# State products of a head in one group, its outputs in another: mLSTM and retention in a hybrid decoder step

## The chip, the cores and the metric

The kernel runs on one core of one Trainium2 chip. The metric is the time of one execution on the device in microseconds (us). Five engines work beside each other, each through a queue of its own in program order, and wait for each other by semaphores: PE (TensorE, the matrix multiplier; its weight loads are listed as PEld), DVE (VectorE), ACT (ScalarE), POOL (GpSimd) and SP (SyncE, which here issues nearly all DMAs).

## The reference, cut to what matters

One decoder layer is run for a prompt of 512 tokens and for 8 samples of 8 tokens, 576 token columns in all. The input is projected by a wide matrix; four token mixers (RWKV-7, sliding-window attention, mLSTM, retention: branches a, b, c, d) work on parts of the projection; each branch output is gated, multiplied by its own matrix `w_branch[i]`, weighted and summed, and one output projection and a layer norm follow. The change concerns the two mixers with a matrix state:

```python
# mLSTM, per chunk (decays, stabilisers and normalisers left out)
A = jnp.einsum('bqhd,bkhd->bhqk', qc, kc) * wts
num = jnp.einsum('bhqk,bkhv->bhqv', A, vc) + sc[..., None] * jnp.einsum('bqhd,bhdv->bhqv', qc, C)
C_new = s_old[..., None, None] * C + jnp.einsum('bhk,bkhd,bhkv->bhdv', wj, kc, vc)
...
# retention, per chunk
inner = jnp.einsum('bqhd,bkhd->bhqk', qc, kc) * decay_mat
o = (jnp.einsum('bhqk,bkhv->bqhv', inner, vc)
     + jnp.einsum('bqhd,bhdv->bqhv', qc, S) * q_dec.T[None, :, :, None])
S = c_dec[None, :, None, None] * S + jnp.einsum('bkhd,bkhv,hk->bhdv', kc, vc, k_dec)
...
# after the branches
for i, y_i in enumerate((y_a, y_b, y_c, y_d)):
    branch = (y_i * z[:, :, i]).astype(x.dtype) @ w_branch[i]
    merged = merged + gate[:, :, i] * branch
out = merged.astype(x.dtype) @ w_out
```

## The kernel before

**Stages.** The prompt's 512 tokens are cut into four chunks of 128; the samples' 64 tokens are a fifth. The large dense products run in blocks. A block of the input projection is 128 output rows by 576 tokens over 16 slices of the inner dimension; each slice takes six matmuls (a high and a low half of both operands, three products, times two column halves), so a block is 96 matmuls into the tile `psd`. A block of a branch product (`w_branch`) has 8 slices and 48 matmuls, also into `psd`; it is written w*n*_*c* here, with *n* the branch and *c* one of its 16 blocks. Ahead of each four slices ACT splits the weights (`wh`) and DVE takes the rest (`wl`), in three buffers each (line 1584 on).

The order of the stages is: branches a, b and c, beside which input blocks run; then `Seven` (line 1264), which computes the remaining input blocks in pairs by a seven-product scheme, into the tile `pmx`, 168 matmuls a pair in place of 2 x 96; then branch d, beside which the blocks of w0 and w1 run; then what is left of the 64 branch blocks; and last the output projection (`pso`).

**What sets the order.** PE takes its matmuls in program order. `S.pump(n)` (`pump`, in `hybrid_kernel`) puts *n* steps into PE's stream, each step one slice (six matmuls) of the dense block at hand, and lets every pending finishing piece advance by a step. The counts in the pump calls of `branch_c_heads`, `branch_d` and `head_out` therefore decide how much dense work stands between the small matmuls of a head, and how far the list `work` has come when a branch ends. When branch c ends, all input blocks but four that were not yet begun go to `Seven`; the number of pairs follows from that (`rest`, then `n = (len(names) - AFTER_SEVEN) // 2`). `S.need(x)` pumps until x is done. The order of instructions on ACT, DVE and SP is set when the program is built, by a scheduler that follows the dependences.

**A head.** Branch c has 8 heads in 4 pairs, branch d has 8 heads. A head computes scores (`k2` by `q2`, `kr` by `qr`), multiplies them by decays (`at`), and then, chunk by chunk: the output from the scores (`vt`, `at`), to which the state of the chunk before is added (`cn`, `qd` or `dst`, `qd`), an eviction by ACT into `o`, the state product (`vt`, `kt`), and the new state by DVE (`cn`, `dst`). Two pump steps stand at each chunk. In branch c the outputs use the array as 128x128, the state term as 64x128 and the state product as 128x64 (rows by columns). The fifth chunk follows, and `head_out` normalises `o` (DVE statistics, POOL's `pow`, DVE), pumps 10 steps and transposes the result (`c_ident`, `o`) for `y`, which goes to DRAM (`yd`).

**Rows of a branch.** Before w*n*_0 can run, `load_rows` must bring branch n's 8 rows from DRAM (`ya<-yd`, `yb<-zsd`, two buffers each), multiply them (DVE `ya`), and split them (ACT `yh`, DVE `yl`). Rows 0 to 2 of branch 1 are asked for at w0_8, the others at the end of w0; those of branch 2 are asked for right after branch d's code, whatever block is at hand:

```python
    branch_d(S)
    rows.mixing = False
    y2ctx = ctx.enter_context(ExitStack())
    y2 = y2ctx.enter_context(tc.tile_pool(name="y2", bufs=1, side="right", reuse_waits="tile"))
    load_rows(2, range(8), y2)
    while current or work or finishing:
        pump(1)
```

## Time and profile before

| what | us |
|---|---|
| median of 3 runs (3237.12 to 3242.02) | 3240.61 |
| the profiled execution | 3245.12 |
| its span, first to last instruction | 3243.4 |
| PE busy in the span | 3194.1 |
| DVE busy | 1916.4 |
| ACT busy | 1190.1 |
| mean granted clock of TensorE | 0.992 |

The profiled execution is 4.5 us above the median and 3.1 us above the slowest of the three runs; 1.7 us of its time lie outside the span. In the views a row with `x2` merges two instructions. A matrix multiplication of plain 32-bit operands appears as two matmuls in the trace, so a head's `vt,at` stands there as `x2`. In "idle before" and in the view of waits, the name behind the arrow is what ended the wait. The clock column gives the TensorE clock that was granted, 1.00 being full speed.

### The profile page before, as it was taken

To read this page: it belongs to the slowest core of one execution; us is meant where nothing else is said; L and a number is where in the kernel's file an instruction comes from. 1 tells how busy PE (TensorE), PEld (TensorE's weight loads), DVE (VectorE), ACT (ScalarE), POOL (GpSimd) and SP (SyncE) were. 2 spreads that over 40 slices of the span, in tenths; PEclk is the share of its full clock that TensorE was granted. 3 is DMA by queue.
4 is the path that set the end of the run, shared out by engine and by line. 5 is a ranking of instruction groups with operands and counts; after the bars stand their busy time and mean duration, and the time that the engine had idled before them with its cause. 6 is when DMAs were issued, how large, how long until landed. Compare 5 with 4: busy or idle time off the path is not lost.

```text
span 3243.4 us, 60432 instructions
## 1 busy us (share of the span) xinstructions
PE 3194.1 (98%) x24238; PEld 3055.5 (94%) x24238; DVE 1916.4 (59%) x3889; ACT 1190.1 (37%) x2453; POOL 361.2 (11%) x606
## 2 busy tenths in 40 slices
PE   8999999999999999999999999999999999899998
PEld 8999999999999999999999999999999999899886
DVE  5555655665543663566566666666665676555426
ACT  4333433333232443323244444444444232223211
POOL 0432243224301220000000000000000000000000
PEclk9999999999999999999999999999999999899999
DMA  5332322323234222432443333333335774554513
GB/s 161 100 90 82 98 79 81 93 85 92 80 98 138 81 89 90 142 111 87 152 131 123 122 120 124 121 124 123 117 124 175 242 228 149 165 173 130 184 60 111
DMA packets 185017, 395.19 MB, mean 122 GB/s; under 512 B 64472, under 2 KB 69336, under 8 KB 184144
## 3 DMA queue, kind: packets, MB, share of 16 engines
q1 hardware_dynamic: 184736, 391.32, 38.2%
q8 instruction: 191, 3.13, 0.4%
q14 instruction: 90, 0.74, 0.1%
HBM read 323.99 MB, written 65.59 MB: 120 GB/s over the span
## 4 chain that ended last, share of the span: by engine, by line
PE 92%; DMA 3%; DVE 3%; ACT 1%; issue 1%; SPq 0%; POOL 0%; ACTq 0%; DVEq 0%; POOLq 0%
PE psd L1484 47%; PE pmx L1484 26%; PE pm L1484 13%; PE pso L1532 6%; DMA xs<-in_xT 1%; DVE wl L1590 1%; DMA raw<-in_wi 1%; ACT wh L1589 0%; DMA ya<-yd 0%; DVE xk L1500 0%; DMA raw<-in_wo 0%; DVE tm L1500 0%; DVE e L1500 0%; DVE res L1500 0%; DMA raw<-in_wb 0%
## 5 line engine op out<-in xcount | busy, mean ns | idle before, releaser
L1590 DVE TENSOR_TENSOR wl<-raw,wh 128x512 fp32r<-128x512 f32 x740 | 535.3, 726 | 467.9 <-ACT wh L1589 452.8
L1589 ACT ACTIVATE wh<-raw 128x512 fp32r<-128x512 f32 x740 | 465.0, 630 | 921.3 <-PE psd L1484 691.3
L1484 PE MATMUL psd<-xh,wh 128*128 128x288 f32 (+2 forms) x3072 | 707.6, 312 | 9.8 <-ACT wh L1589 9.4
L1484 PE MATMUL psd<-xl,wh 128*128 128x288 f32 (+2 forms) x3072 | 660.2, 296 | 0.0
L1484 PE MATMUL psd<-xh,wl 128*128 128x288 f32 (+2 forms) x3072 | 659.3, 296 | 0.4 <-DVE wl L1590 0.4
L1484 PEld LDWEIGHTS psd<-xh,wh 128*128 128x128 f32 x3072 | 492.0, 189 | 38.4 <-issue 12.6
L1484 PEld LDWEIGHTS psd<-xh,wl 128*128 128x128 f32 x3072 | 504.4, 189 | 1.2 <-DVE wl L1590 1.0
L1484 PEld LDWEIGHTS psd<-xl,wh 128*128 128x128 f32 x3072 | 504.5, 189 | 0.0
L1484 PE MATMUL pmx<-xh,wl 128*128 128x288 f32 x1248 | 369.0, 296 | 3.5 <-DVE wl L1590 3.5
L1484 PE MATMUL pmx<-xl,wh 128*128 128x288 f32 x1248 | 368.8, 295 | 0.0
L1484 PE MATMUL pmx<-xh,wh 128*128 128x288 f32 x1248 | 368.8, 295 | 0.0
L1484 PE MATMUL pmx<-fh,wl 128*128 128x288 f32 x864 | 257.5, 298 | 0.0
L1484 PE MATMUL pmx<-fl,wh 128*128 128x288 f32 x864 | 255.4, 296 | 0.0
L1484 PE MATMUL pmx<-fh,wh 128*128 128x288 f32 x864 | 254.4, 294 | 0.0
L1484 PEld LDWEIGHTS pmx<-xh,wl 128*128 128x128 f32 x1248 | 235.9, 189 | 3.9 <-DVE wl L1590 3.9
L1484 PE MATMUL psd<-yh,wh 128*128 128x288 f32 x1024 | 227.2, 304 | 11.1 <-ACT yh L1500 8.8
L1484 PEld LDWEIGHTS pmx<-xh,wh 128*128 128x128 f32 x1248 | 236.0, 189 | 0.0
L1484 PEld LDWEIGHTS pmx<-xl,wh 128*128 128x128 f32 x1248 | 235.8, 189 | 0.0
L1484 PE MATMUL psd<-yl,wh 128*128 128x288 f32 x1024 | 221.3, 298 | 0.3 <-DVE yl L1500 0.3
L1484 PE MATMUL psd<-yh,wl 128*128 128x288 f32 x1024 | 221.2, 298 | 0.0
L1484 POOL TENSOR_TENSOR rstd<-rstd,mhalf 128x5 f32<-128x5 f32 (+1 forms) x24 | 37.5, 1565 | 1567.1 <-DVE rstd L1500 1567.1
L1484 PEld LDWEIGHTS psd<-yh,wh 128*128 128x128 f32 x1024 | 165.5, 191 | 14.4 <-ACT yh L1500 9.7
(384 smaller groups left out, 4957.1 us busy)
## 6 DMA issues: line engine op xcount, KB each, us to landing
raw<-in_wi SPq DMA_DIRECT2D x270, 512.0 KB
sraw<-in_wi SPq DMA_DIRECT2D x72, 512.0 KB
raw<-in_wb SPq DMA_DIRECT2D x64, 512.0 KB
gd<-zs SPq DMA_DIRECT2D x64, 288.0 KB
th<-gd SPq DMA_DIRECT2D x64, 288.0 KB
raw<-in_wo SPq DMA_DIRECT2D x32, 512.0 KB
zsd<-zs SPq DMA_DIRECT2D x32, 288.0 KB
ya<-yd SPq DMA_DIRECT2D x32, 288.0 KB
```

The costliest lines, as they stand in the source:

```text
L1484: ins = f(*a, **k).ins
L1532: PE.matmul(out=out, lhsT=lhsT, rhs=rhs, start=start, stop=stop)
L1589: a = nc.scalar.activation(out=wh, in_=src, func=ACTF.Copy)
L1590: b = nc.vector.tensor_tensor(out=wl, in0=src, in1=wh.bitcast(FP32), op=ALU.subtract)
```

## The change

In both branches the four state products of a head are issued as one group of matmuls, ahead of the outputs, into banks shared by several chunks; DVE then computes the four states in a row; after some pump steps the four outputs (with the state terms) are issued as a second group, and ACT evicts several chunks with one instruction (three and one in branch c, four in branch d). Branch d keeps a head's four states in one tile. The pump counts change with it: in branch c a head pumped 4, four times 2, and 10 in `head_out`, 22 in all, and now 2, 5, 2 and 10, or 19; in branch d it pumped 6, 1, 3, four times 2 and 10, 28 in all, and now 6, 1, 2, 4, 2 and 7, or 22.

```diff
 FILL_BONUS = 10
+FILL_HEAD = dict(c=10, d=7)
...
                 V.memset(at[64:P, 4, 0:64], 0.0)
-                S.pump(4)
+                S.pump(2)
+
+                ps = [pm() for _ in range(2)]
+                inc = [ps[c // 3][rs, 129 * (c % 3):129 * (c % 3) + 129] for c in range(4)]
+                for c in range(4):
+                    mm(inc[c], kt[:, c, rs], vt[:, c, e])
+                for c in range(4):
+                    pst = inc[c]
+                    if c:
+                        stt(cn[c][rs], cn[c - 1][rs], scb[rs, c * P + P - 1:c * P + P], pst, ALU.mult, ALU.add)
+                    else:
+                        V.tensor_copy(out=cn[c][rs], in_=pst)
+                S.pump(5)
+                ps = [pm() for _ in range(2)]
                 for c in range(4):
                     cs = slice(c * P, c * P + P)
-                    S.pump(2)
-                    po = pm()
-                    mm(po[:, 0:129], at[:, c], vt[:, c, e], stop=(c == 0))
+                    po = ps[c // 3][:, 129 * (c % 3):129 * (c % 3) + 129]
+                    mm(po, at[:, c], vt[:, c, e], stop=(c == 0))
                     if c:
-                        mm(po[:, 0:129], qd[rs, cs], cn[c - 1][rs], start=False)
-                    act(o[:, c], po[:, 0:129])
-                    pst = pm()
-                    mm(pst[rs, 0:129], kt[:, c, rs], vt[:, c, e])
-                    if c:
-                        stt(cn[c][rs], cn[c - 1][rs], scb[rs, c * P + P - 1:c * P + P], pst[rs, 0:129], ALU.mult, ALU.add)
-                    else:
-                        V.tensor_copy(out=cn[c][rs], in_=pst[rs, 0:129])
+                        mm(po, qd[rs, cs], cn[c - 1][rs], start=False)
+                act(o[:, 0:3], ps[0][:, 0:387].rearrange("p (c v) -> p c v", c=3))
+                act(o[:, 3], ps[1][:, 0:129])
+                S.pump(2)
...
-            S.pump(3)
-
+            S.pump(2)
+
+            pst = pm()
+            for c in range(4):
+                mm(pst[:, c * P:c * P + P], kt[:, c], vt[:, c])
+            st = pool.tile([P, 4, P], FP32, tag="dst", name="dst", bufs=2)
+            V.tensor_copy(out=st[:, 0], in_=pst[:, 0:P])
+            for c in range(1, 4):
+                stt(st[:, c], st[:, c - 1], GAM128[h], pst[:, c * P:c * P + P], ALU.mult, ALU.add)
+            S.pump(4)
             o = pool.tile([P, 5, P], FP32, tag="o", name="o", bufs=2)
-            st = None
+            po = pm()
             for c in range(4):
                 cs = slice(c * P, c * P + P)
-                po = pm()
-                mm(po[:, 0:P], at[:, c], vt[:, c], stop=(c == 0))
+                mm(po[:, cs], at[:, c], vt[:, c], stop=(c == 0))
                 if c:
-                    mm(po[:, 0:P], qd[:, cs], st, start=False)
-                act(o[:, c], po[:, 0:P])
-                pst = pm()
-                mm(pst[:, 0:P], kt[:, c], vt[:, c])
-                new = pool.tile([P, P], FP32, tag="dst", name="dst", bufs=3)
-                if c:
-                    stt(new, st, GAM128[h], pst[:, 0:P], ALU.mult, ALU.add)
-                else:
-                    V.tensor_copy(out=new, in_=pst[:, 0:P])
-                st = new
-                S.pump(2)
+                    mm(po[:, cs], qd[:, cs], st[:, c - 1], start=False)
+            act(o[:, 0:4], po.rearrange("p (c d) -> p c d", c=4))
+            S.pump(2)
+            st = st[:, 3]
...
-    S.pump(10)
+    S.pump(FILL_HEAD[which])
```

The order of instructions moves at three places that the prediction speaks of. A row below has its number on the engine, the line, the operation, the tiles written and read, and the size; xN stands for N equal rows, and lines behind the changed heads are 9 higher in the changed kernel.

The first place is PE in branch d's first head, one chunk before:

```order
13627 L1484 MATMUL psd<-yh,wl 128x288 x2
13628 L1484 MATMUL pm<-vt,at 128x128
13629 L1484 MATMUL pm<-dst,qd 128x128
13630 L1484 MATMUL pm<-vt,kt 128x128
13631 L1484 MATMUL psd<-yh,wh 128x288 x2
```

The same head of the changed kernel on PE, first its state products, then its outputs:

```order
13646 L1493 MATMUL psd<-yl,wh 128x288 x2
13647 L1493 MATMUL psd<-yh,wl 128x288 x2
13648 L1493 MATMUL pm<-vt,kt 128x128 x4
13649 L1493 MATMUL psd<-yh,wh 128x288 x2
13650 L1493 MATMUL psd<-yl,wh 128x288 x2
```

```order
13660 L1493 MATMUL psd<-yh,wl 128x288 x2
13661 L1493 MATMUL pm<-vt,at 128x128 x2
13662 L1493 MATMUL pm<-dst,qd 128x128
13663 L1493 MATMUL pm<-vt,at 128x128
13664 L1493 MATMUL pm<-dst,qd 128x128
13665 L1493 MATMUL pm<-vt,at 128x128
13666 L1493 MATMUL pm<-dst,qd 128x128
13667 L1493 MATMUL psd<-yh,wh 128x288 x2
```

The same eleven small matmuls stand in two groups with four pump steps (24 matmuls) between them, where they stood in four groups with two steps between.

The second place is PE at the two ends of `Seven`: the last input block before it, its first matmuls, its last one and the first branch block, before:

```order
7159 L1484 MATMUL psd<-xl_135,wh 128x288 x2
7160 L1484 MATMUL psd<-xh_134,wl 128x288 x2
7161 L1484 MATMUL pmx<-xh_80,wh 128x288
7162 L1484 MATMUL pmx<-xl_81,wh 128x288
13496 L1484 MATMUL pmx<-xh_134,wl 128x288
13497 L1484 MATMUL psd<-yh,wh 128x288 x2
```

The same place of the changed kernel:

```order
7031 L1493 MATMUL psd<-xl_135,wh 128x288 x2
7032 L1493 MATMUL psd<-xh_134,wl 128x288 x2
7033 L1493 MATMUL pmx<-xh_80,wh 128x288
7034 L1493 MATMUL pmx<-xl_81,wh 128x288
13536 L1493 MATMUL pmx<-xh_134,wl 128x288
13537 L1493 MATMUL psd<-yh,wh 128x288 x2
```

Every row from the first `pmx` to the last is one matmul: 6336 before and 6504 now, one pair (168) more; the input blocks in `psd` lose 192 matmuls of 288 columns, two blocks.

The third place is ACT from the `y` of branch d's last head on (`yh<-ya` are the rows of branch 2, `wh` the weights of the branch blocks), before:

```order
1770 L1589 ACTIVATE wh<-raw 128x512 x2
1771 L1500 ACTIVATE y<-pm,pp 128x512
1772 L1500 ACTIVATE y<-pm,pp 128x64
1773 L1589 ACTIVATE wh<-raw 128x512
1774 L1500 ACTIVATE yh<-ya 128x576 x2
1775 L1589 ACTIVATE wh<-raw 128x512
1776 L1500 ACTIVATE yh<-ya 128x576 x2
1777 L1589 ACTIVATE wh<-raw 128x512
1778 L1500 ACTIVATE yh<-ya 128x576 x4
1779 L1589 ACTIVATE wh<-raw 128x512 x13
```

The same place of the changed kernel:

```order
1755 L1598 ACTIVATE wh<-raw 128x512 x2
1756 L1509 ACTIVATE y<-pm,pp 128x512
1757 L1509 ACTIVATE y<-pm,pp 128x64
1758 L1598 ACTIVATE wh<-raw 128x512
1759 L1509 ACTIVATE yh<-ya 128x576 x2
1760 L1598 ACTIVATE wh<-raw 128x512 x2
1761 L1509 ACTIVATE yh<-ya 128x576 x2
1762 L1598 ACTIVATE wh<-raw 128x512 x2
1763 L1509 ACTIVATE yh<-ya 128x576 x2
1764 L1598 ACTIVATE wh<-raw 128x512 x2
1765 L1509 ACTIVATE yh<-ya 128x576 x2
1766 L1598 ACTIVATE wh<-raw 128x512 x21
```

The eight rows of branch 2 now have two weight splits between each pair of rows. On PE the last head's transposes stand inside block w1_15 before, with 36 of its matmuls behind them and then w2_0; now they stand inside w1_9, with 36 of its matmuls behind them, then w1_10 to w1_15 whole, and then w2_0.

## The prediction

> **What bounds the kernel now.** I read the page first (busy times, then the chain), then the windows by stage, then PE's waits.
>
> ```profile
> span 3243.4 us, 60432 instructions
> PE 3194.1 (98%) x24238; PEld 3055.5 (94%) x24238; DVE 1916.4 (59%) x3889; ACT 1190.1 (37%) x2453; POOL 361.2 (11%) x606
> PE 92%; DMA 3%; DVE 3%; ACT 1%; issue 1%; SPq 0%; POOL 0%; ACTq 0%; DVEq 0%; POOLq 0%
> ```
>
> PE is busy for 98% of the span and is 92% of the chain that ended last. So a microsecond is won only where PE gets fewer matmuls, where a matmul takes less of PE's stream, or where PE stands still. The next view says where it stands still. Its columns are the stretch, its length, then busy time and count of PE, PEld, DVE, ACT and POOL, the granted clock, the DMA share and GB/s. The first row is branch c's heads, the second branch d with its blocks, the third w2_0 and w2_1, the fourth two later blocks of w2, the last the stretch from w2_2 to the output projection.
>
> ```profile
> 1360.00:1600.00 240.00, 239.86 (x1801) 220.43 (x1800) 153.46 (x492) 72.86 (x162) 9.39 (x8) 1.00 0.31 97
> 2509.00:2798.50 289.50, 287.18 (x2189) 278.35 (x2189) 189.64 (x410) 77.76 (x164) 9.75 (x8) 0.99 0.61 199
> 2798.50:2826.70 28.20, 19.12 (x99) 17.38 (x98) 14.09 (x20) 6.59 (x11) 0.00 (x0) 0.70 0.65 205
> 2839.50:2852.30 12.80, 12.80 (x99) 12.80 (x98) 5.43 (x8) 2.53 (x5) 0.00 (x0) 1.00 0.42 129
> 2826.70:3018.70 192.00, 192.00 (x1443) 192.00 (x1442) 108.15 (x172) 56.58 (x91) 0.00 (x0) 1.00 0.48 152
> ```
>
> In the heads that the change rewrites PE idles 0.14 us (240.00 - 239.86) and 2.3 us (289.50 - 287.18). There is hardly a wait to remove there. The hole lies behind them: the same 99 matmuls take 28.20 us in the third row and 12.80 us in the fourth, 15.4 us more. The waits of PE name it:
>
> ```profile
> PE psd L1484 <- ACT wh L1589: 11.7, 5, 6.8
> PE psd L1484 <- ACT yh L1500: 8.8, 3, 3.1
> PE pmx L1484 <- DVE wl L1590: 3.5, 2, 2.4
> ```
>
> Three waits for `yh` are 8.8 us: w2_0 needs the rows of branch 2, which are asked for only after branch d. ACT's rows in that place, with start, length and in brackets the idle time before:
>
> ```profile
> 2793.48 1.07 ACT L1500 ACTIVATE y<-pm,pp 128x512 f32<-128x512 f32 x2 [1.67 <-PE pm L1484]
> 2795.21 0.63 ACT L1589 ACTIVATE wh<-raw 128x512 fp32r<-128x512 f32 x1 [0.65 <-PE psd L1484]
> 2795.74 1.25 ACT L1500 ACTIVATE yh<-ya 128x576 fp32r<-128x576 f32 x2
> 2798.46 0.63 ACT L1589 ACTIVATE wh<-raw 128x512 fp32r<-128x512 f32 x1 [1.47 <-issue]
> 2802.58 1.40 ACT L1500 ACTIVATE yh<-ya 128x576 fp32r<-128x576 f32 x2 [3.50 <-DVE ya L1500]
> 2805.97 0.63 ACT L1589 ACTIVATE wh<-raw 128x512 fp32r<-128x512 f32 x1 [1.99 <-PE psd L1484]
> 2808.69 1.35 ACT L1500 ACTIVATE yh<-ya 128x576 fp32r<-128x576 f32 x2 [2.09 <-DVE ya L1500]
> 2814.92 1.36 ACT L1500 ACTIVATE yh<-ya 128x576 fp32r<-128x576 f32 x2 [4.88 <-DVE ya L1500]
> ```
>
> Two rows come every 6.1 to 6.2 us (2802.58, 2808.69, 2814.92), since two buffers go round through a DMA; the last pair ends at 2816.28, 22.8 us after the `y` of the last head. The other 6.6 us of the 15.4 are clock:
>
> ```profile
> 2803.32 0.53 PE L1484 MATMUL psd<-yh,wh 128*128 128x288 f32 x2 [3.08 <-ACT yh L1500]
> 2811.34 0.68 PE L1484 MATMUL psd<-yh,wh 128*128 128x288 f32 x2
> 2811.82 0.68 PE L1484 MATMUL psd<-yl,wh 128*128 128x288 f32 x2
> ```
>
> After the idle 3.08 us two matmuls are 0.48 us apart from the next two (2811.34, 2811.82), where 192.00 us for 1443 matmuls is 0.1331 us each, 0.27 for two. The Trainium skill says of this ("TensorE: Matmul & The Clock Gate", Part 1) that the array's clock is halved after an idle window of about 3.4 us and restored after a busy one. The row agrees, nearly twice the spacing at a granted 0.70 over the window.
>
> **The change part by part.**
>
> *Pump counts in branch c, 22 to 19 a head.* 24 steps less let the list of input blocks come less far, and the order shows the result: two blocks (192 matmuls in `psd`) go over to one more pair of `Seven` (168 in `pmx`). One row gives the pace there:
>
> ```profile
> 1700.00:2400.00 700.00, 700.00 (x5268) 700.00 (x5267) 469.18 (x659) 342.58 (x627) 0.00 (x0) 1.00 0.38 122
> ```
>
> 700.00 / 5268 = 0.1329 us. 192 x 0.1331 = 25.6 us go and 168 x 0.1329 = 22.3 us come: **-3.2 us**. The pair's additions lie on DVE, 67% busy there (469.18 of 700), and cost nothing while PE never waits in this stretch.
>
> *Grouping in branch d.* One chunk on PE:
>
> ```profile
> 2646.36 0.38 PE L1484 MATMUL pm<-vt,at 128*128 128x128 f32 x2
> 2646.58 0.39 PE L1484 MATMUL pm<-dst,qd 128*128 128x128 f32 x2
> 2646.81 0.39 PE L1484 MATMUL pm<-vt,kt 128*128 128x128 f32 x2
> 2646.95 0.51 PE L1484 MATMUL psd<-yh,wh 128*128 128x288 f32 x2
> 2648.61 0.39 PE L1484 MATMUL pm<-vt,at 128*128 128x128 f32 x2
> ```
>
> A round is 2.25 us (2646.36 to 2648.61); its 12 dense matmuls are 12 x 0.1331 = 1.60, the six small ones 0.65, 0.11 each, just their spacing inside the group (0.22 for two). Going in and out of the dense stream costs nothing visible, so the same 22 small matmuls a head cost the same in two groups: **0**, bounds 0.05 us for each of the 16 groups saved, 0.8 either way.
>
> *Grouping in branch c.* The same round, with the array's shape in the fifth place:
>
> ```profile
> 1458.70 0.39 PE L1484 MATMUL pm<-vt,at 128*128 128x129 f32 x2
> 1459.01 0.49 PE L1484 MATMUL pm<-cn,qd 64*128 64x129 f32 x2
> 1459.43 0.43 PE L1484 MATMUL pm<-vt,kt 128*64 128x129 f32 x2
> 1459.79 0.53 PE L1484 MATMUL psd<-xh,wh 128*128 128x256 f32 x2
> 1461.48 0.38 PE L1484 MATMUL pm<-vt,at 128*128 128x129 f32 x2
> ```
>
> 2.78 - 1.60 = 1.18 us for six small matmuls, 0.53 more than in branch d, over three changes of shape: 0.18 each. A head changed shape 12 times up to the end of its fifth chunk (2, 3, 3 and 4); now 11 times (into and out of the state products, 6 in the outputs, 3 in the fifth chunk, which used to follow the last state product in its shape). 8 x 0.18 = **-1.4 us**. Bounds: if the eight passes of the products run at 0.11 as in branch d, 0.42 a head or -3.4 is saved; if the new entry costs 0.18 and nothing is saved, +1.4. I take the count. The Trainium skill has a rule that speaks against hoping for more here ("TensorEngine Tiling (Array Packing)", Tiling Modes, Key Properties): a change of tiling mode drains the array. The two groups of rows agree, and by that rule the outputs, which still alternate two shapes, keep their cost.
>
> *The states on DVE.* The four states must now be there before the output group.
>
> ```profile
> L1500 DVE SCALAR_TENSOR_TENSOR cn<-cn,scb,pm x24: 337/350/359, 1376.0 to 1585.8; 64x129 f32<-64x129 f32 x24
> L1500 DVE SCALAR_TENSOR_TENSOR dst<-dst,pm x24: 251/282/290, 2547.9 to 2779.1; 128x128 f32<-128x128 f32 x24
> ```
>
> With the first copy that is about 4 x 0.35 = 1.4 us in branch c under five steps (5 x 6 x 0.1331 = 4.0 us) and 4 x 0.28 = 1.1 us in branch d under four (3.2 us): about 2 us to spare even with one weight split of 0.7 between. **0**. ACT's fewer evictions lie beside PE: 0.
>
> *`head_out` in branch d pumps 7 instead of 10*, 3 x 0.80 = 2.4 us less cover for the normalisation. Its end and the transposes that need it, in the last head and in the fifth (where rows of branch 1 are loaded):
>
> ```profile
> 2786.18 1.11 DVE L1500 TENSOR_SCALAR o<-o,hmv,rstd 128x128 f32<-128x128 f32 x4
> 2792.84 0.80 PE L1484 MATMUL pm<-c_ident,o 128*128 128x128 f32 x5
> 2660.88 0.33 DVE L1500 TENSOR_SCALAR o<-o,hmv,rstd 64x128 f32<-64x128 f32 x1
> 2663.26 0.80 PE L1484 MATMUL pm<-c_ident,o 128*128 128x128 f32 x5
> ```
>
> 5.5 us of slack in the last head become 3.1. In the fifth 2.05 become -0.35: **+0.4 us**, up to +3 if the rows of branch 1 slip as well.
>
> *Pump counts in branch d, 28 to 22 a head.* This is the large term. 8 x 6 = 48 steps are six branch blocks: the last head now ends in w1_9, and 36 + 6 x 48 = 324 matmuls (43.1 us) stand between its transposes and w2_0, where 36 (4.8 us) stood. The rows need 22.8 us from there; nothing else holds w2_0, so the stall and its slow clock go: **-15.4 us**. What is late next there is the weight split, since the rows' waits stand in ACT's queue ahead of `wh`. But ACT writes a `wh` when PE frees its buffer (0.65 <- PE), two groups of 24 matmuls (6.4 us) before it is used, and the new order puts two `wh` (6.4 us of PE) between pairs of rows that come every 6.2 us.
>
> **Sum:** -3.2 - 1.4 + 0.4 - 15.4 = -19.6 us. On the profiled execution 3245.1 - 19.6 = 3225.5 us; that one was 4.5 us over the median, so on the median 3240.6 - 19.6 = **3221 us**.
>
> **The rivals.**
>
> 1. *The wait moves to the weights.* If the two groups of lead aren't there, ACT's waits for rows (3.50 + 2.09 + 4.88 = 10.5 us) come back as waits for `wh`: 3231.5 us. For it speaks that `wh` stands behind them in one queue; against it the lead. 10%.
> 2. *The hole stays.* If something other than the late request holds w2_0 (its DMAs behind stores in SP's queue), only the pair, the shapes and the fifth head count: -4.2, 3236.4 us. Against it: the pairs come at an even pace from the request on. 5%.
> 3. *PE waits for the states in every head* (the slower side). DVE takes its queue in order, and it is busy 189.64 of 289.50 us in branch d. If more than about 2 us stand ahead of the state chain, PE waits at the output group; from 1.6 us a head in all 16 heads on (26 us) the gain is gone by over 0.2%. At 2 us a head: 3221 + 32 = 3253 us. Against it: in the old order each state was needed two steps (1.6 us) after its product, and PE lost only 0.14 us in branch c. 4%.
> 4. *Short waits slow the clock.* At w2_0 8.8 us of waiting brought 6.6 us of slow clock, 0.75 us for each. Should each head of branch d come to wait 1 us, 8 x 1.75 = 14 us come back: 3235 us, no change. Against it: with four groups a head the clock stood at 0.99 over branch d. 3%. The Trainium skill knows such a case ("TensorE: Matmul & The Clock Gate", A second HAM failure mode: psum-queue depth-cycling): short idle times between groups of matmuls that go round the banks make the clock swing.
>
> **How the numbers follow.** The forecast has 78%; its own range is 3215 (the -3.4 bound, no wait in the fifth head, the runs' own spread of 2 to 4 us) to 3228 (+1.4, +3, spread). The range takes in rival 1: 3214 to 3233; it leaves out 2, 3, 4 and the forecast's ends. 0.2% is 6.5 us, about what a measurement here tells from no change. Faster by more: forecast and rival 1, 0.88. Within: rivals 2 and 4, 0.08. Slower: rival 3, 0.04.
>
> **What would show it.** In the profile after: `pmx` at 6504 matmuls; no wait of PE for `yh` and full clock where w2_0 and w2_1 run, 12.8 us for the two; a wait below 1 us at the transposes of branch d's fifth head; PE idle below 1 us in branch c. Waits for `wh` between w1_10 and w2_0 would speak for rival 1, waits for `cn` or `dst` ahead of `qd` for rival 3, clock rows below 0.97 in branch d for rival 4.

## The result and the profile after

The changed kernel takes **3224.61 us** (median of 4 runs, 3220.89 to 3227.69); the kernel before, measured beside it, 3241.32 us (3237.12 to 3244.36). The ratio is **0.9948, 95% interval 0.9937 to 0.9960**: half a per cent faster, 16.7 us by the medians. Measured a second time in another job it was 0.9950 (0.9938 to 0.9963). 3221 us had been forecast, with a range of 3214 to 3233.

The page of the changed kernel, span, busy time and chain:

```profile
span 3225.9 us, 60410 instructions
PE 3185.4 (99%) x24214; PEld 3048.7 (95%) x24214; DVE 1921.9 (60%) x3902; ACT 1191.4 (37%) x2423; POOL 362.4 (11%) x606
PE 93%; DMA 3%; DVE 3%; ACT 1%; issue 1%; SPq 0%; POOL 0%; ACTq 0%; DVEq 0%; POOLq 0%
```

PE is still what bounds it. The totals say little about where 17.5 us of span went; for that the program is cut at the same instructions in both traces. Two of the cuts, PE's timeline at the first head's scores of branch c (`pm<-cv`) and at w0_0 (the first `psd<-yh`), before:

```profile
1366.15 1.41 PE L1484 MATMUL pm<-cv 64*128 64x128 f32 x10
...
2509.37 0.42 PE L1484 MATMUL psd<-yh,wh 128*128 128x288 f32 x2
```

and after:

```profile
1367.14 1.41 PE L1493 MATMUL pm<-cv 64*128 64x128 f32 x10
...
2506.66 0.42 PE L1493 MATMUL psd<-yh,wh 128*128 128x288 f32 x2
```

The windows of the changed kernel by stage (columns as in the prediction): branch c's heads, branch d with its blocks, w2_0 and w2_1, two later blocks of w2, and the rest of the blocks:

```profile
1360.00:1600.00 240.00, 238.97 (x1791) 220.40 (x1790) 153.47 (x501) 71.17 (x148) 9.34 (x8) 1.00 0.35 110
2506.66:2798.08 291.42, 288.17 (x2186) 278.26 (x2185) 196.70 (x422) 78.63 (x146) 9.65 (x8) 0.99 0.66 212
2798.08:2810.87 12.79, 12.79 (x98) 12.79 (x97) 5.44 (x8) 2.54 (x5) 0.00 (x0) 1.00 0.40 124
2823.67:2836.47 12.80, 12.80 (x98) 12.80 (x97) 5.44 (x8) 2.54 (x5) 0.00 (x0) 1.00 0.39 134
2810.87:3002.79 191.92, 191.92 (x1442) 191.92 (x1441) 108.39 (x173) 56.95 (x91) 0.00 (x0) 1.00 0.48 153
```

| stage (us) | before | after | difference |
|---|---|---|---|
| start to branch c's first scores (same instructions) | 1366.15 | 1367.14 | +1.0 |
| branch c, the rest of the input blocks, `Seven`, to w0_0 | 1143.22 | 1139.52 | -3.7 |
| w0_0 to w2_0 (branch d with its blocks) | 289.11 | 291.42 | +2.3 |
| w2_0 and w2_1 | 28.21 | 12.79 | -15.4 |
| w2_2 to the end (same instructions) | 416.71 | 415.03 | -1.7 |
| span | 3243.4 | 3225.9 | -17.5 |

The third window is the one to look at: w2_0 and w2_1 now take 12.79 us at full clock, exactly what two later blocks take. The hole is gone whole, its idle time and its slow clock. The first and the last stage hold the same instructions in both kernels, and they differ by 1.0 and 1.7 us; that is the measure for how much a difference of 2 us in one pair of profiles means. The 1.7 us are a matter of the clock: in the profile before, PE ran at a granted clock of 0.50 from 3026.7 to 3030.1 us, which loses 1.7 us, and in the changed kernel's it ran at 1.00 from 3000 to 3040 us.

Why the hole is gone can be seen on ACT, from the last head's `y` on (start, length, idle before):

```profile
2754.99 1.07 ACT L1509 ACTIVATE y<-pm,pp 128x512 f32<-128x512 f32 x2 [1.68 <-PE pm L1493]
...
2757.25 1.25 ACT L1509 ACTIVATE yh<-ya 128x576 fp32r<-128x576 f32 x2
...
2779.91 0.69 ACT L1509 ACTIVATE yh<-ya 128x576 fp32r<-128x576 f32 x1 [1.49 <-DVE ya L1509]
```

The last row of branch 2 is ready at 2780.60, and w2_0 starts at 2798.08: 17.5 us to spare. But the rows take 25.6 us from the `y` (2754.99), where they took 22.8 before. That becomes important below.

### The profile page after: what moved, and what is told of

The parts are those of the page before. It is cut to its first block, busy times and chain, and to the rows that moved or that the text cites. A ratio compares the mean times of both kernels' runs of the same rounds, so it can differ in the third digit from the quotient of the medians.

```text
span 3225.9 us, 60410 instructions
## 1 busy us (share of the span) xinstructions
PE 3185.4 (99%) x24214; PEld 3048.7 (95%) x24214; DVE 1921.9 (60%) x3902; ACT 1191.4 (37%) x2423; POOL 362.4 (11%) x606
## 4 chain that ended last, share of the span: by engine, by line
PE 93%; DMA 3%; DVE 3%; ACT 1%; issue 1%; SPq 0%; POOL 0%; ACTq 0%; DVEq 0%; POOLq 0%
PE psd L1493 47%; PE pmx L1493 27%; PE pm L1493 13%; PE pso L1541 6%; DMA xs<-in_xT 1%; DMA raw<-in_wi 1%; DVE wl L1599 1%; ACT wh L1598 0%; DMA raw<-in_wo 0%; DVE xk L1509 0%; DMA ya<-yd 0%; DVE tm L1509 0%; DMA raw<-in_wb 0%; DVE e L1509 0%; DVE res L1509 0%
## 5 line engine op out<-in xcount | busy, mean ns | idle before, releaser
L1493 PE MATMUL psd<-xh,wh 128*128 128x288 f32 (+1 forms) x3008 | 693.3, 312 | 9.3 <-ACT wh L1598 8.9
L1493 PE MATMUL psd<-xl,wh 128*128 128x288 f32 (+1 forms) x3008 | 646.6, 296 | 0.0
L1493 PE MATMUL psd<-xh,wl 128*128 128x288 f32 (+1 forms) x3008 | 645.4, 296 | 0.0
L1493 PEld LDWEIGHTS psd<-xh,wh 128*128 128x128 f32 x3008 | 482.6, 190 | 35.9 <-issue 9.8
L1493 PEld LDWEIGHTS psd<-xh,wl 128*128 128x128 f32 x3008 | 494.3, 189 | 0.4 <-DVE wl L1599 0.2
L1493 PEld LDWEIGHTS psd<-xl,wh 128*128 128x128 f32 x3008 | 494.4, 189 | 0.0
L1493 PE MATMUL pmx<-xh,wh 128*128 128x288 f32 x1280 | 378.2, 295 | 2.0 <-ACT wh L1598 2.0
L1493 PE MATMUL pmx<-xh,wl 128*128 128x288 f32 x1280 | 378.5, 296 | 1.0 <-DVE wl L1599 1.0
L1493 PE MATMUL pmx<-xl,wh 128*128 128x288 f32 x1280 | 378.1, 295 | 0.0
L1493 PE MATMUL pmx<-fh,wl 128*128 128x288 f32 x888 | 264.6, 298 | 0.0
```

What stands on the lines that cost most here:

```text
L1493: ins = f(*a, **k).ins
```

## The experiments

All ratios are to the kernel before, measured in the same job, with 95% intervals. Unless something else is said, an edit is made to the changed kernel.

**1. The grouping alone.** Both branches' groups, with the pump totals of before (22 steps a head in branch c, 28 in branch d):

```
 branch c: S.pump(2), S.pump(5), S.pump(2)  ->  S.pump(3), S.pump(5), S.pump(4)
 branch d: S.pump(2), S.pump(4), S.pump(2)  ->  S.pump(3), S.pump(5), S.pump(3)
-FILL_HEAD = dict(c=10, d=7)
+FILL_HEAD = dict(c=10, d=10)
```

> The grouped heads of the changed kernel with the old totals of pump steps (branch c 3, 5, 4 and 10 = 22 a head; branch d 6, 1, 3, 5, 3 and 10 = 28). The order shows 6336 matmuls in pmx and the last head inside w1_15, as before. Theory 1 (the gain comes from where the dense blocks end up, the grouping itself is worth nothing): the time of before within 3 us, about 3241 us, and w2_0 with w2_1 again near 28 us in place of 12.8. Theory 2 (the grouping itself takes waits or shape changes off PE): most of the gain stays, about 3225 us, with or without the hole at w2_0.

Measured: 3241.16 us, ratio 1.0006 (0.9997 to 1.0015). The hole is back, as the window of w2_0 and w2_1 and PE's waits show:

```profile
2798.88:2826.85 27.97, 18.52 (x99) 16.90 (x98) 14.28 (x20) 6.63 (x11) 0.00 (x0) 0.76 0.66 206
```

```profile
PE psd L1493 <- ACT yh L1509: 9.2, 3, 4.0
```

PE's timeline at the two cuts of branch c:

```profile
1367.34 1.41 PE L1493 MATMUL pm<-cv 64*128 64x128 f32 x10
...
2510.78 0.42 PE L1493 MATMUL psd<-yh,wh 128*128 128x288 f32 x2
```

From branch c's first scores to w0_0 it is 1143.44 us, 0.2 more than before (1143.22), with the same steps and the same pairs. In branch d a head takes 32.5 us from its scores to those of the next head, before 32.4. The grouping, which gives the change its name, is worth nothing on PE that can be measured in either branch.

**2. The counts alone.** The heads as before, four groups each, with the totals of the changed kernel (19 and 22 steps):

```
 branch c: S.pump(4), 4 x S.pump(2)  ->  S.pump(2), S.pump(2 if c < 3 else 1) per chunk
 branch d: S.pump(3), 4 x S.pump(2)  ->  S.pump(3), S.pump((2, 2, 1, 0)[c]) per chunk
-    S.pump(10)
+    S.pump(FILL_HEAD[which])      # c=10, d=7
```

> The heads of before, chunk by chunk, with the new totals (branch c 2, 2, 2, 2, 1 and 10 = 19; branch d 6, 1, 3, 2, 2, 1, 0 and 7 = 22). The order shows 6504 matmuls in pmx and the last head inside w1_9, as in the changed kernel. Theory 1: the time of the changed kernel, 3222 to 3226 us, no wait of PE for yh at w2_0, and w2_0 with w2_1 at 12.8 us; the shorter distances between a state and its use may cost up to 1 us a head in branch d's last two chunks. Theory 2: 3238 us, since only the pair of the seven-product stage is won.

Measured: 3226.83 us, ratio 0.9963 (0.9950 to 0.9975). The window of w2_0 and w2_1:

```profile
2800.80:2813.60 12.80, 12.80 (x99) 12.80 (x98) 5.44 (x8) 2.53 (x5) 0.00 (x0) 1.00 0.39 130
```

They take 12.80 us, with no wait for `yh`. The large term belongs to the counts. This kernel has one weak place of its own: w1_0 takes 16.51 us, with 2.0 us of waiting for `yl` and a granted clock of 0.90 there, where the changed kernel has 13.04 us and 0.3. From branch c's first scores to w0_0 it took 1141.47 us, of which 1.7 were lost in a stretch at half clock (from 1468.6 us) that the changed kernel's profile doesn't have; without it the stage is as long as the changed kernel's (1139.52). The ratio is 0.0015 above the changed kernel's, and the intervals overlap; so the grouping may have helped a little to bear the lower counts, but that isn't shown.

**3. Branch c alone.** Branch c as changed, branch d and its `head_out` as before:

```
 branch d: as in the kernel before, S.pump(10) in head_out
```

> Branch c as in the changed kernel, branch d as before with its 28 steps a head (head_out 10 for both). pmx has 6504 matmuls, the last head ends inside w1_15. Theory 1: only the pair is won, 3.2 us less about 1 us for a wait of PE for ACT's y that the changed kernel shows in branch c: 3238 to 3240 us, the hole at w2_0 whole (28 us for w2_0 and w2_1). Theory 2: branch c's grouping wins its 1.4 us or more on top, 3236 us or less. By the rows of branch c: theory 1 expects the matmuls of products, outputs and fifth chunk to take 6.4 us a head as before, theory 2 at least 0.18 less.

Measured: 3238.73 us, ratio 1.0004 (0.9995 to 1.0013): no gain that can be measured. From branch c's first scores to w0_0 it took 1141.70 us, 1.5 less than before, and the hole behind it 29.26 us, 1.0 more (before 28.21). The pair of `Seven` is there (6504 matmuls in `pmx`), but alone it drowns in the scatter.

**4. Only the request late.** 48 steps are pumped behind the last head, ahead of the request for the rows:

```
     rows.mixing = False
+    pump(48)
     ...
     load_rows(2, range(8), y2)
```

> The changed kernel with one line more: 48 pump steps (six branch blocks) between the end of branch d and the request for the rows of branch 2, so that 36 matmuls stand between the request and w2_0, as before the change. Nothing else moves. Theory 1: the hole comes back whole, 3224.6 + 15.4 = 3240 us, with three waits for yh of about 9 us in all and a granted clock near 0.7 over w2_0 and w2_1. Rival (the hole went because the heads of branch d leave ACT, DVE or the DMA queue freer): 3225 to 3229 us.

Measured: 3237.75 us, ratio 0.9994 (0.9985 to 1.0003): by the ratios 0.9994 - 0.9948 = 0.0046, some 15 us of the gain are lost again, each ratio being uncertain by about 0.001. The window of w2_0 and w2_1:

```profile
2793.65:2818.06 24.41, 19.36 (x98) 16.95 (x97) 12.26 (x18) 5.84 (x10) 0.00 (x0) 0.72 0.69 217
```

Everything up to the last head is as in the changed kernel. Moving one request behind six blocks brings back 11.6 us of hole (24.41 - 12.79). That is not the whole hole that was expected: PE waits twice for `yh`, 4.7 us in all, where about 9 us had been forecast. The first two rows are split 7.5 us ahead of w2_0 here (ACT's `yh` at 2786.13), before only 2.7 us ahead (2795.74), where they followed the last head's `y` by 2.3 us; here that `y` stands 35.6 us earlier (2750.56). What the change gained at w2_0, it gained by asking earlier.

**5. Almost no cover for the states.** One step between products and outputs, the others behind the outputs:

```
 branch c: S.pump(2), S.pump(5), S.pump(2)  ->  S.pump(2), S.pump(1), S.pump(6)
 branch d: S.pump(2), S.pump(4), S.pump(2)  ->  S.pump(2), S.pump(1), S.pump(5)
```

> The changed kernel, but with one pump step (6 matmuls, 0.80 us) between a head's state products and its outputs, where branch c had five and branch d four; the steps taken there are pumped behind the outputs, so that each head's total, the blocks and the pair stay as they were. It measures how much of the cover the states on DVE really need (rival 3 of the prediction). Theory (the states are DVE's copy and three additions in a row, 4 x 0.35 = 1.4 us in branch c and 4 x 0.28 = 1.1 us in branch d, behind the product's own latency and at times a weight split): PE waits for cn or dst in most of the 16 heads, about 1 us in c and 0.5 us in d, 12 us in all, with clock rows below 0.99 in those heads: 3225 + 12 to + 20 = 3237 to 3245 us, ratio about 1.000. Rival (the order on PE inside the output group is itself cover, since the first products at, vt come ahead of the first state and the later states are asked for later): waits below 0.4 us a head, 3225 to 3231 us.

PE's waits for states in the whole program:

```profile
PE pm L1493 <- DVE dst L1509: 1.1, 4, 0.6
```

None for `cn`, four for `dst`, 1.1 us in all, where the theory had 12. The rival is right: the outputs begin with products that need no state, and each later state is asked for later, so that the order inside the group is cover itself. The time was 3228.15 us, ratio 0.9969 (0.9956 to 0.9981), 6 to 7 us more than the changed kernel by the ratios, with intervals that overlap a little. The waits for states explain 1.1 us of it. The profiled execution was the slowest of the five (3235.05 us), and its span is 7.4 us longer than the changed kernel's. Of these, 2.7 us lie ahead of branch c, in instructions that weren't touched. Another 2.6 lie between branch c's first scores and w0_0: a longer wait for `wl` (1.9 us in place of 1.0), and a stretch of half clock (granted 0.50 from 1474.2 to 1477.4 us) that loses 1.7 and that the changed kernel's profile doesn't have. The last 1.9 us lie behind w2_1, where another such stretch stands (0.50 from 3017.0 to 3020.3 us). So nothing of the profile's difference but the 1.1 us points at the states; what made the other runs longer isn't known.

**6. Four blocks back in front.** 26 steps a head in branch d:

```
-FILL_HEAD = dict(c=10, d=7)
+FILL_HEAD = dict(c=10, d=11)
```

> The changed kernel, but head_out in branch d pumps 11 steps instead of 7: 26 steps a head, 32 more in all, so that four of the six branch blocks go back in front of the last head. Behind the last head's transposes stand 36 + 2 x 48 = 132 matmuls (17.6 us) ahead of w2_0, where the changed kernel has 324 and the kernel before 36. Theory (a threshold: the last pair of rows comes 22.8 us after the last head's y and is used three quarters into w2_0, 4.8 us after its start, so w2_0 may start from 18 us on): w2_0 and w2_1 wait 0 to 2 us, 13 to 16 us for the two, the fifth head's wait of 0.9 us at its transposes is gone (11 steps cover the normalisation): 3224 to 3227 us, ratio 0.995. Rival (each block taken out of the heads bought its share of the gain, 15.4 / 6 = 2.6 us): four blocks give 10.3 us back, 3235 us, ratio 0.998.

Measured: 3236.73 us, ratio 0.9993 (0.9984 to 1.0002). The time is near the rival's, but not for its reason. The windows of w1_0 and of w2_0 with w2_1, and PE's waits:

```profile
2648.53:2666.30 17.77, 11.87 (x66) 10.47 (x64) 12.01 (x20) 5.57 (x9) 0.00 (x0) 0.71 0.85 261
2801.33:2820.29 18.96, 16.53 (x99) 15.42 (x98) 8.96 (x13) 4.45 (x8) 0.00 (x0) 0.82 0.68 209
```

```profile
PE psd L1493 <- ACT yh L1509: 7.4, 4, 4.3
```

There are two holes. At w2_0 it is 6.2 us (18.96 - 12.79): the last row ended 26.5 us after the last head's `y`, not 22.8. And at w1_0 PE stood 5.9 us (17.77 - 11.87) at a clock of 0.71, a place that neither theory had looked at. The head that this falls into took 40.4 us from its scores to those of the next one, its neighbours 30.9. By the program the last five rows of branch 1 go into tiles that w0_15 still reads. With these counts the end of w0_15 falls into a dense stretch of a head, and w1_0 goes on at once to the slices that need those rows; in the kernel before the small matmuls of a head's fifth chunk stand ahead of w1_0, and in the changed one they stand behind its first slice. That these give the rows their time is read from the order; no run tests it alone.

**7. Without the pair.** Branch c at 22 steps a head, branch d as changed:

```
 branch c: S.pump(2), S.pump(5), S.pump(2)  ->  S.pump(3), S.pump(5), S.pump(4)
```

> The changed kernel with branch c's pump counts back at 22 a head (3, 5, 4 and 10; grouped heads, branch d as changed): one pair of Seven less (6336 matmuls in pmx), two input blocks more, no hole. It prices the pair by itself. Theory (192 matmuls at 0.1331 us come for 168 at 0.1329 us): w0_0 starts 3.2 us later than in the changed kernel, the time is 3.2 us longer, 3227.5 to 3228.5 us, ratio about 0.996; nothing else moves. Rival (the pair's 168 additions on DVE or its place cost PE what the 24 matmuls save): 3224 to 3225 us, ratio 0.995 and no later w0_0.

Measured: 3226.12 us, ratio 0.9959 (0.9947 to 0.9972), beside 0.9948 and 0.9950 for the changed kernel: 3 to 4 us by the point values, inside the intervals. The trace says more. PE's timeline at the two cuts of branch c:

```profile
1369.10 1.04 PE L1493 MATMUL pm<-cv 64*128 64x128 f32 x7
...
2512.02 0.42 PE L1493 MATMUL psd<-yh,wh 128*128 128x288 f32 x2
```

1142.92 us. The three profiles with 6336 matmuls in `pmx` have 1143.22, 1143.44 and 1142.92, mean 1143.2; the six with branch c exactly as changed 1139.52, 1140.07, 1140.21, 1140.48, 1139.43 and 1141.70, mean 1140.2. The pair is worth 3.0 us.

**8. Branch c in order of the array's shape.** The same matmuls; the fifth chunk's product goes to the state products, and the outputs run by shape:

```
                 for c in range(4):
                     mm(inc[c], kt[:, c, rs], vt[:, c, e])
+                p5 = pm()
+                mm(p5[0:64, 0:129], at[:, 4, 0:64], vt[:, 4, e], stop=False)
...
-                    mm(po, at[:, c], vt[:, c, e], stop=(c == 0))
-                    if c:
-                        mm(po, qd[rs, cs], cn[c - 1][rs], start=False)
+                    mm(po, at[:, c], vt[:, c, e], start=(c % 3 == 0), stop=False)
+                for c in range(1, 4):
+                    mm(ps[c // 3][...], qd[rs, cs], cn[c - 1][rs], start=False, stop=(c > 1))
+                for b in range(8):
+                    mm(p5[0:64, 0:129], qm[rs, b], cn0[rs, b], start=False, stop=(b == 7))
```

> The changed kernel with branch c's small matmuls put in order of the array's shape: the fifth chunk's product of at and vt (128*64) goes behind the four state products (128*64); in the outputs all four at, vt (128*128) come first, then the three qd, cn (64*128), then the fifth chunk's eight qm, scn (64*64); its own group is gone. The same matmuls and the same steps, but 5 changes of the array's shape a head instead of 11. Theory 1 (a change of shape costs 0.18 us, a pass in any shape 0.11): 10 passes and 2 changes, then 30 passes and 3 changes are 1.46 + 3.84 = 5.3 us a head instead of 6.42, 8 x 1.1 = 9 us less: 3216 us, ratio about 0.992. Theory 2 (the cost lies in the passes of the smaller shapes, 0.15 us for a state product, whatever stands beside them; this is how the grouping of branch c can have saved nothing): no gain, 3223 to 3227 us. Rival 3 (states and outputs are asked for in one block, and PE waits at the first qd): a wait for cn before qd, 3225 us or more.

Measured: 3220.47 us, ratio 0.9938 (0.9924 to 0.9951). PE's timeline of one head's outputs (start, length, the array's shape in the seventh place), first in the changed kernel:

```profile
1375.42 0.61 PE L1493 MATMUL pm<-vt,at 128*128 128x129 f32 x4
1375.95 0.49 PE L1493 MATMUL pm<-cn,qd 64*128 64x129 f32 x2
1376.37 0.49 PE L1493 MATMUL pm<-vt,at 128*128 128x129 f32 x2
1376.79 0.49 PE L1493 MATMUL pm<-cn,qd 64*128 64x129 f32 x2
1377.21 0.49 PE L1493 MATMUL pm<-vt,at 128*128 128x129 f32 x2
1377.63 0.49 PE L1493 MATMUL pm<-cn,qd 64*128 64x129 f32 x2
1378.04 0.54 PE L1493 MATMUL psd<-xh,wh 128*128 128x256 f32 x2
```

and in order of shape:

```profile
1378.14 1.05 PE L1495 MATMUL pm<-vt,at 128*128 128x129 f32 x8
1379.12 0.93 PE L1495 MATMUL pm<-cn,qd 64*128 64x129 f32 x6
1379.99 1.98 PE L1495 MATMUL pm<-scn,qm 64*64 64x129 f32 x16
1381.90 0.53 PE L1495 MATMUL psd<-xh,wh 128*128 128x256 f32 x2
```

The same 14 passes take 2.62 us alternating (1375.42 to 1378.04) and 1.85 us sorted (1378.14 to 1379.99). Alternating, each pair of passes takes 0.42 us; sorted, eight `at` passes take 0.98 us, 0.12 each. Over all groups of a head it is 5.31 us in place of 6.42 on the average (counted up to the return into the dense stream), as theory 1 had it (5.3). The outputs with the fifth chunk take 3.86 us in every head. The group of the products took three different times: 1.43 us in two heads, as forecast (1.46); 1.93 in two others, where PE also waited 0.3 us for `at` from DVE; and only 1.22 in the second head of each pair, as much as the eight passes of the state products alone took in the changed kernel. There the two passes of the fifth chunk run beside the others:

```profile
1395.60 0.77 PE L1495 MATMUL pm<-vt,kt 128*64 128x129 f32 x5
1396.10 0.32 PE L1495 MATMUL pm<-vt,at 128*64 128x129 f32 x1
1396.21 0.27 PE L1495 MATMUL pm<-vt,kt 128*64 128x129 f32 x1
1396.26 0.27 PE L1495 MATMUL pm<-vt,at 128*64 128x129 f32 x1
1396.32 0.38 PE L1495 MATMUL pm<-vt,kt 128*64 128x129 f32 x2
```

By the program the state products of a pair's second head go to partitions 64 to 127 and the fifth chunk's product to 0 to 63, while in the first head both go to 0 to 63. So two products of 128x64 that write different halves ran at the same time here. That the average meets 5.3 so closely is luck in part, since this gain and the waits for `at` cancel. The eight heads of branch c take 205.76 us in place of 213.81, 8.1 us less. Of these, 2.1 us are lost again in `Seven` (871.88 us in place of 869.76), where PE waits for `wl` in `pmx` 4.1 us in the whole program in place of 1.0. Whether that belongs to the new places of the blocks or to the scatter is open: the changed kernel's own order gave 869.70 to 871.94 there, and experiment 10, with the same order in branch c, has 2.2 us of such waits.

**9. Three blocks back in front, in the last head only.** This tells the two holes of experiment 6 apart:

```
-    S.pump(FILL_HEAD[which])
+    S.pump(FILL_HEAD[which] + (24 if (which, h) == ("d", 7) else 0))
```

> The changed kernel, but the head_out of branch d's last head alone pumps 31 steps instead of 7: three branch blocks stand in front of its transposes instead of behind them, 36 + 3 x 48 = 180 matmuls (24.0 us) lie between the transposes and w2_0, and everything up to this head is as in the changed kernel (in the kernel with 26 steps a head the place of w1_0 moved too, and PE waited there). Theory (a threshold, with the rows' pace as the changed kernel's trace has it: the last pair of rows ends 25.6 us after the last head's y and is used 4.8 us into w2_0, so w2_0 may start from 20.8 us on): no hole, 12.8 us for w2_0 and w2_1, 3224 to 3227 us, ratio 0.995. Rival (each matmul of cover buys its share, 6.2 us of hole at 132 matmuls and none at 324): 4.6 us of hole, 17.4 us for the two blocks, 3229 us, ratio 0.9965.

Measured: 3225.30 us, ratio 0.9958 (0.9944 to 0.9973). The window of w2_0 and w2_1:

```profile
2794.65:2807.44 12.79, 12.79 (x99) 12.79 (x98) 6.10 (x9) 3.05 (x6) 0.00 (x0) 1.00 0.70 221
```

No hole with 180 matmuls of cover, 6.2 us with 132 and 15.2 with 36 (experiment 1): above a threshold more cover brings nothing, and below it the hole grows; the six blocks have no equal price each. Here w2_0 started 24.0 us after the `y` (2770.66), and the last row ended 24.6 us after it, just in time for its use 4.8 us into w2_0.

**10. The sorted branch c, and a longer cover for the normalisation.** Experiment 8 with

```
 branch d: S.pump(2), S.pump(4), S.pump(2)  ->  S.pump(2), S.pump(2), S.pump(1)
-FILL_HEAD = dict(c=10, d=7)
+FILL_HEAD = dict(c=10, d=10)
```

> The kernel with branch c's small matmuls in order of the array's shape, and in branch d three of the steps between products, outputs and fifth chunk moved behind the normalisation (2, 2, 1 and 10 in place of 2, 4, 2 and 7; totals unchanged). The short cover run had at most 1.1 us of waits for states in branch d with one step there. Expected: the fifth head's wait of 0.9 us at its transposes goes, no wait for dst above 0.3 us, branch c as in the merged kernel (5.3 us a head for its groups): 3217 to 3221 us, ratio 0.992 to 0.994, faster than the changed kernel by 4 to 7 us in the same job. Against it: the weights' waits in pmx, 4.1 us in the merged kernel's profile beside 1.0 in the changed one's, belong to the new places of the blocks and stay; then 3 us are left of it.

and beside it the changed kernel itself:

> The changed kernel itself, once more, for a comparison within one job: 3224.6 us median by the first measurement, ratio 0.995. It also shows how much one stage scatters between two profiles of the same instructions: from w0_0 to w2_0 it took 291.4 us in the first profile, and 286.9 us for the same instructions in the kernel that only pumps behind the last head. If that is scatter, this profile lies between 286 and 292.

Measured: **3219.01 us**, ratio 0.9932 (0.9918 to 0.9945), beside 3225.24 us and 0.9950 (0.9938 to 0.9963) for the changed kernel. It is the fastest of all, 6.2 us below the changed kernel by the medians, though the two intervals still overlap a little. The fifth head's normalisation is ready 6.1 us ahead of its transposes; one wait for `dst` of 0.5 us came in its place, a little more than expected.

## Why the prediction was right

**The branch blocks (-15.4): right in kind and size.** 28.21 us became 12.79. Experiment 2 shows that the counts do it without the grouping, experiment 4 that a late request alone brings most of it back, experiments 6 and 9 that it is a threshold. One number in the working was too low: the rows needed 24.6 to 26.5 us from the `y` in the nine profiles where PE worked most of that time or all of it, not the 22.8 us read in the old trace, where PE stood still (22.6 and 23.8 in experiments 1 and 3, which have the same hole). Why they are slower beside a busy PE isn't shown. With 43.1 us of cover it made no difference here; with 17.6 us (experiment 6) it decided.

**The pair of `Seven` (-3.2): right**, 3.0 us by nine profiles. No single ratio could have shown it (experiments 3 and 7).

**Grouping in branch d (0): right**, by the heads of experiment 1 (32.5 us, before 32.4).

**Grouping in branch c (-1.4): mis-sized, it measured 0.** The step that failed is the count of changes of shape at 0.18 us each, from 12 to 11 a head. Taken from the last dense matmul ahead of a group to the sixth behind it, less the dense ones' own spacing, a head's groups had 0.79 + 2 x 1.20 + 3.22 = 6.41 us (median over the heads), and have 1.22 + 2.73 + 2.47 = 6.42. The price per change is about right on the average (six changes fewer a head gave 1.1 us in experiment 8, with the two effects named there), but with 0.11 us for a pass these groups give between 0.15 (24 passes and 4 changes in 3.22 us) and 0.20 (14 passes and 6 changes in 2.73 us), so that a difference of one change can't be forecast from it.

**The states on DVE (0): right, with more room than thought.** "About 2 us to spare" was too careful, by experiment 5.

**The fifth head's normalisation (+0.4): right.** The head beside which rows of branch 1 are loaded is the fifth in the changed kernel; in the kernel before it is the fourth, and the prediction's transposes at 2663.26 us, called the fifth head's, are the fourth of the eight. The end of the normalisation on DVE and the transposes on PE in the changed kernel:

```profile
2670.43 1.36 DVE L1509 TENSOR_SCALAR o<-o,hmv,rstd 128x128 f32<-128x128 f32 x5 [0.39 <-POOL rstd L1493]
```

```profile
2670.93 1.22 PE L1493 MATMUL pm<-c_ident,o 128*128 128x128 f32 x5
```

The five transposes take 1.22 us in place of 0.80, since they wait inside for the last rows of `o` (0.92 in experiment 4, with the same instructions). The stage as a whole became 2.3 us longer, though. From its scores to those of the next head, a head of branch d takes 27.6 to 27.7 us, before 32.4; the first head took 29.2, before 33.3, and the fifth 29.2. So 0.6 us of the 2.3 lie in the first head, whose wait for `wh` and slow clock (below) were there before and were longer now, which no term had. And 1.5 us lie in the fifth, 0.4 of them at the transposes and about 0.9 at waits for rows of branch 1, which the prediction had as a bound (up to +3) and not as a term. A new wait of 0.9 us in branch c for ACT's `y` wasn't in the sum either; with it PE idles 1.03 us in the window of branch c, just above the 1 us that the prediction had named as a sign.

**The sum.** -19.6 was forecast, -17.5 came in the profile and -16.7 in the medians. By the table the profile is 0.9 us short in the stage of branch c (-3.7, forecast -4.6) and 1.9 us in that of branch d (+2.3, forecast +0.4); the two stages with the same instructions give 0.7 us back.

**The rivals.** No wait for `wh` between w1_10 and w2_0 (each of the six blocks 6.3 to 6.4 us): rival 1 falls. The hole didn't stay: rival 2 falls. PE waits for no state: rival 3 falls, and experiment 5 shows that one step in place of five or four hardly brings it about. The clock stands at 0.99 over branch d, as before, and at 0.97 over the 60 us around its first head in both kernels: rival 4 falls.

## What to carry to other kernels

When work is woven into a loop in program order, the counts decide which transfers are asked for how early; look where the next data are requested, count the work between that place and its first use, and compare it with the time that the transfer takes beside a busy engine, not in the stall (here 24.6 to 26.5 us, not 22.8). Such cover is a threshold: above it more brings nothing, below it the wait comes with a slow clock on top, and a cut that clears one boundary can move another (w1_0 in experiment 6). Regrouping small matmuls on PE pays where it takes many changes of the array's shape away (six a head, 8 us here), not by making groups larger.

## What the hardware showed unexpectedly

**Short waits are enough to halve the clock.** PE's timeline in w2_0 of experiment 6 (in brackets the idle time before):

```profile
2807.98 0.54 PE L1493 MATMUL psd<-yh,wh 128*128 128x288 f32 x2 [1.70 <-ACT yh L1509]
2808.77 0.54 PE L1493 MATMUL psd<-yl,wh 128*128 128x288 f32 x2 [0.26 <-DVE yl L1509]
...
2810.16 0.85 PE L1493 MATMUL psd<-yh,wh 128*128 128x288 f32 x2 [0.47 <-ACT yh L1509]
...
2815.43 0.68 PE L1493 MATMUL psd<-yl,wh 128*128 128x288 f32 x2
2815.91 0.53 PE L1493 MATMUL psd<-yh,wl 128*128 128x288 f32 x2
2816.28 0.43 PE L1493 MATMUL psd<-yh,wh 128*128 128x288 f32 x2
```

Waits of 1.70 and 0.26 us, and from 2809.3 us on the clock is halved (a third wait of 0.47 falls into that): two matmuls take 0.48 us (2815.43 to 2815.91) until 2816, where two take 0.27 elsewhere. In the first head of branch d one wait for `wh` tells the two cases apart. PE's waits from 2500 to 2560 us and the window there, in the changed kernel:

```profile
PE psd L1493 <- ACT wh L1598: 2.8, 1, 2.8
```

```profile
2500.00:2560.00 60.00, 57.15 (x421) 55.40 (x420) 34.37 (x69) 13.39 (x27) 1.17 (x1) 0.97 0.78 250
```

and in the kernel of experiment 9, whose instructions are the same up to there:

```profile
PE psd L1493 <- ACT wh L1598: 0.9, 1, 0.9
```

```profile
2500.00:2560.00 60.00, 58.91 (x444) 57.18 (x443) 37.62 (x75) 14.57 (x30) 1.17 (x1) 1.00 0.81 268
```

A wait of 2.8 us brought the clock to 0.97 over the window, one of 0.9 us didn't touch it. So it was at this place in all thirteen profiles: with a wait of 2.3 to 2.9 us (four of them) the window has 0.97, with one of 0.9 to 1.7 us (nine) 1.00. The length of the wait doesn't decide it everywhere: in branch c PE waits 0.9 us for ACT's `y` between small matmuls of 64x64 (`vt,km`) in eight profiles, and in two of them (experiments 2 and 5) a stretch of half clock follows, in six none. The Trainium skill ("TensorE: Matmul & The Clock Gate", Part 1) has the slow clock come after an idle window of about 3.4 us; these waits were all shorter.

**The slow clock doesn't cost in proportion to the stall.** Beyond the idle time itself the hole cost 6.2 - 2.4 = 3.8 us in experiment 6, 11.6 - 5.1 = 6.5 us in experiment 4, and 15.2 - 9.5 = 5.7 us in experiment 1 (idle is the window's length less PE's busy time). In these traces the half clock comes in stretches of 3.4 us or a multiple of it: 3.4 us in the first head of the changed kernel (from 2537.8 us), 6.8 us at w2_0 in experiment 6 (from 2809.3), 13.6 us in experiment 1 (from 2808.4). A stretch of 3.4 us in which PE is busy loses 1.7 us.

**The same instructions scatter by some microseconds.** Ahead of branch c, where all the kernels are the same, PE reached the first scores between 1364.70 and 1369.89 us in thirteen profiles. From w0_0 to w2_0 the changed kernel took 291.42 us and in its second profile 291.50; experiments 4 and 9, with the same instructions up to the last head, took 286.86 and 287.67. In experiment 4, 3.2 of the 4.6 us lie up to the end of the first head, with its wait for `wh` and the clock, and 1.4 in the fifth. So the 2.3 us by which that stage grew are within its scatter. A term of 1 to 3 us is read from its own stage and from several profiles, not from a span.
